# Hybrid conv and neighbourhood-attention layer on one core: weights planned one projection ahead, attention in 48 groups of four blocks

## The chip, the core and the metric

The kernel runs on one core of a Trainium2 chip. The metric is the device time of one execution in microseconds (us). TensorE is called PE here, VectorE DVE, ScalarE ACT, GpSimd POOL, and SyncE, which issues most of the transfers, SP.

## The reference, cut to what matters

One layer on 512 prompt tokens and 1024 sample tokens (d = 1024), with 16 meta tokens ahead of them. The normalised input goes through one projection into seven parts; a gated depthwise convolution of 31 taps and an attention over a neighbourhood of 8 rows by 16 columns work on these, and their gated results are projected back.

```python
u = rms_norm(h, pre_g)
z = jnp.einsum('bld,de->ble', u, w_in)
c_val, c_glu, c_gate, q, k, v, a_gate = jnp.split(z, [...])
conv_out = conv_module(c_val, c_glu, ...) * silu(c_gate)   # val*sigmoid(glu) -> 31 taps -> LayerNorm -> silu
o_meta, o_grid = neighbourhood_attention(q, k, v, ...)      # softmax over window and meta keys
att = concat(o_meta, o_grid).reshape(B, L, D_ATT) * silu(a_gate)
mixed = concat([conv_out, att], -1)
return h + rms_norm(einsum('ble,ed->bld', mixed, w_out), post_g)
```

## The kernel before, in words

All operands are fp32. Projections run in fp32r with every operand split into a high part (a cast on ACT) and a low part (a difference on POOL or DVE), so each product is three matmuls: high by high, low by high, high by low. In a fp32 matmul (transposes `tp`, weighted values `po`) the trace shows two passes for each instruction.

The stages follow each other: normalisation and transposes of the input (to about 160 us), the conv stage (160 to 692), attention (to about 1235), the handover and the output stage (to 1516).

Projection weights come in sets of 128 output columns. `load_w(ec)` (L118 to L126 and the lines it calls) loads set `ec` into `wraw` (DMA on SP, L122), ACT casts it into `whi` (L115), POOL subtracts into `wlo` (L116). Each of the three has two buffers. `proj` (L133) then does 24 matmuls for up to 512 tokens: that is called a unit here. A set serves three or four units. Sets 0 to 7 are conv values, 8 to 15 conv gates (`glu`), 16 to 23 the gates of the conv branch, 24 to 31 Q, 32 to 39 K, 40 to 47 the gates of the attention branch.

In the conv stage, channel block `c` (of 8) is filtered by DVE: 30 instructions of `scalar_tensor_tensor` (L223) on `z`, each 128 x 1536, and a first one on ACT (L221). While DVE filters block `c`, PE does filler units (`v_units`, `c_gate`, `a_gate`, about 44 us of them per chunk) and then gate and value units of block `c + 1` (`conv_proj`). A chunk ends by time, so a gate's three units may be cut over two chunks. The last block, c = 7, is filtered in two parts (`LASTP`): segment 0 alone (512 wide), then segments 1 and 2 (1024 wide). After a pass, `conv_stats` makes `zc` on DVE, `zq` on ACT and sums on POOL (for c = 7's second part on DVE). Matmuls with `ones` (L423) then sum over the partitions.

Attention goes pair by pair (8 pairs of heads): K of the pair (four units, L478 to L487 split it), then for each of three token groups Q (one unit, L514, L515) and `attention`, which for each of eight query blocks does scores `ss` on PE (L548, three matmuls of high and low parts), the softmax on DVE and ACT (L556 to L561), transposes `tp` (L564), their copy `pT` (ACT, L566) and the weighted values `po` (L571). `po` of a group is one PSUM bank of eight blocks; `mo` copies it out (L574) and L575 stores it. PSUM: three banks `mm`, two `ss`, two `tp`, one `po`. `pt` has three buffers, `pT` two.

The order on each engine is not the program's: a scheduler picks among the ready instructions, earlier ones in the program first, and fixes each engine's order when the kernel is built. So the units of a later Q or K stand between the blocks of an earlier group. At the end, `mix` loads gates and results (L645, L646), makes `mh` and `ml` (L654, L655), and the output product `py` (L682) runs on weights that `load_wo` loads and splits (L616, L626, L627).

## Time and profile before

| | us |
|---|---|
| median of three runs | 1517.15 |
| the runs | 1515.48, 1517.20, 1517.15 |
| the profiled execution | 1517.83 |
| its span, first to last instruction | 1516.1 |
| PE busy | 1460.5 (96%) |
| DVE busy | 1006.9 (66%) |
| ACT busy | 585.3 (39%) |
| POOL busy | 351.4 (23%) |

PE's share is near the whole span in every stage; the other engines wait for it most of the time. To be read from the profile are therefore PE's waits with what ended each, the stages' busy times, and the starts of PE's instructions one after the other: matmuls overlap, so the price of one is the time from its start to the start of the next, and its own length in a row is longer.

### The profile page before, as it was taken

The numbers are of one execution on the slowest core, as the hardware profiler recorded it, in microseconds if no ns is written. First come the engines' busy times: TensorE is split into PE (matmuls) and PEld (weight loads), VectorE is DVE, ScalarE is ACT, GpSimd is POOL, SyncE is SP. The second block draws the span as 40 slices with busy tenths as digits, with TensorE's granted clock in tenths as the row PEclk, the third lists the DMA queues.
The fourth block names the chain that finished last, engine by engine and source line by source line (L and its number), as shares of the span: only waits on it lengthen the run. The fifth ranks groups of instructions, "written<-read, shape, count | busy, mean of one in ns | idle before, by whom it ended". The sixth has DMA issues, their size and how long they took to land.

```text
span 1516.1 us, 24156 instructions
## 1 busy us (share of the span) xinstructions
PE 1460.5 (96%) x9506; PEld 1241.3 (82%) x9506; DVE 1006.9 (66%) x1739; ACT 585.3 (39%) x1296; POOL 351.4 (23%) x258
## 2 busy tenths in 40 slices
PE   7998999999999898969999999999999979999998
PEld 6987898989988787757888888888887867888876
DVE  7699989797959698991545545546555557553442
ACT  7312121122111121112544545545544567456652
POOL 1133232233031323562121111111210002122121
PEclk9999999999999999989999999999999999999999
DMA  8013123141122131024112222212222367454542
GB/s 274 24 49 104 46 59 112 53 137 61 48 74 90 38 103 63 29 87 122 52 56 65 63 61 82 66 44 61 86 58 81 119 189 218 131 169 131 148 137 75
DMA packets 124470, 138.91 MB, mean 92 GB/s; under 512 B 8110, under 2 KB 96430, under 8 KB 124356
## 3 DMA queue, kind: packets, MB, share of 16 engines
q1 hardware_dynamic: 124356, 137.36, 29.6%
q8 instruction: 75, 1.23, 0.3%
q14 instruction: 39, 0.32, 0.1%
HBM read 99.05 MB, written 42.71 MB: 94 GB/s over the span
## 4 chain that ended last, share of the span: by engine, by line
PE 76%; DVE 9%; DMA 6%; issue 4%; POOL 2%; ACT 2%; SPq 0%; DVEq 0%; POOLq 0%; ACTq 0%
PE mm L133 49%; PE mm L286 8%; DVE z L223 5%; PE ss L548 5%; PE po L571 5%; PE tp L564 4%; PE py L682 4%; DMA mb<-std 2%; DMA mx<-zs 2%; POOL wlo L116 1%; POOL ml L655 1%; DMA yo<-in_wo 1%; DVE mx L653 1%; DVE mx L649 1%; DVE mx L648 1%
## 5 line engine op out<-in xcount | busy, mean ns | idle before, releaser
L133 PE MATMUL mm<-uw,whi 128*128 128x512 f32 (+2 forms) x2688 | 757.2, 364 | 3.2 <-ACT whi L115 3.2
L133 PEld LDWEIGHTS mm<-uw,whi 128*128 128x128 f32 x2688 | 485.1, 190 | 83.7 <-ACT whi L115 4.9
L223 DVE SCALAR_TENSOR_TENSOR z<-ub,cw_sb,z 128x1536 f32<-128x1536 f32 (+2 forms) x300 | 507.7, 1710 | 23.4 <-ACT z L221 15.2
L133 PE MATMUL mm<-uw,wlo 128*128 128x512 f32 (+2 forms) x1344 | 488.4, 364 | 18.1 <-POOL wlo L116 18.1
L133 PEld LDWEIGHTS mm<-uw,wlo 128*128 128x128 f32 x1344 | 255.6, 190 | 56.8 <-POOL wlo L116 19.1
L116 POOL TENSOR_TENSOR wlo<-wraw,whi 128x1024 fp32r<-128x1024 f32 x48 | 150.0, 3126 | 437.9 <-ACT whi L115 433.0
L682 PE MATMUL py<-uw,mh 128*128 128x512 f32 x576 | 180.0, 394 | 6.8 <-ACT mh L654 6.2
L286 PE MATMUL mm<-vh,uw 128*128 128x256 f32 x768 | 141.9, 284 | 1.1 <-ACT uw L158 0.6
L566 ACT COPY pT<-tp 108x256 f32<-108x256 f32 (+4 forms) x192 | 76.1, 425 | 153.4 <-PE tp L564 146.9
L682 PEld LDWEIGHTS py<-uw,mh 128*128 128x128 f32 x576 | 108.8, 189 | 31.1 <-ACT mh L654 6.4
L286 PEld LDWEIGHTS mm<-vh,uw 128*128 128x128 f32 x768 | 119.4, 190 | 3.3 <-ACT uw L158 1.0
L559 ACT ACTIVATE pt<-pt,sm 128x216 f32<-128x216 f32 (+4 forms) x192 | 96.9, 505 | 46.3 <-DVE sm L558 44.6
L682 PE MATMUL py<-uw,ml 128*128 128x512 f32 x288 | 113.2, 394 | 0.8 <-POOL ml L655 0.8
L556 DVE CUSTOM_DVE_ANT_0 pt<-ss,ei 128x216 f32<-128x216 f32 (+2 forms) x144 | 60.8, 439 | 77.7 <-PE ss L548 73.7
L655 POOL TENSOR_TENSOR ml<-mx,mh 128x1024 fp32r<-128x1024 f32 x22 | 54.4, 2490 | 245.5 <-ACT mh L654 245.5
L286 PE MATMUL mm<-vl,uw 128*128 128x256 f32 x384 | 108.1, 282 | 0.0
L561 DVE TENSOR_SCALAR pt<-pt,sm 128x216 f32<-128x216 f32 (+4 forms) x192 | 76.2, 397 | 5.5
L564 PE MATMUL tp<-ident,pt 128*96 128x128 f32 (+2 forms) x480 | 78.8, 282 | 0.0
L286 PEld LDWEIGHTS mm<-vl,uw 128*128 128x128 f32 x384 | 72.7, 189 | 0.8 <-issue 0.5
L115 ACT CAST whi<-wraw 128x1024 fp32r<-128x1024 f32 x48 | 50.3, 1048 | 48.9 <-PE mm L133 32.8
L571 PEld LDWEIGHTS po<-pT,vt 96*64 96x64 f32 (+1 forms) x1408 | 47.8, 137 | 23.5 <-issue 13.4
L682 PEld LDWEIGHTS py<-uw,ml 128*128 128x128 f32 x288 | 54.4, 189 | 13.6 <-POOL ml L655 1.3
(147 smaller groups left out, 1630.7 us busy)
## 6 DMA issues: line engine op xcount, KB each, us to landing
wraw<-in_w_main SPq DMA_DIRECT2D x48, 512.0 KB
xt<-in_xn SPq DMA_DIRECT2D x12, 512.0 KB
vd<-vs SPq DMA_DIRECT2D x96, 64.0 KB
zs<-zc SPq DMA_DIRECT2D x24, 256.0 KB
cgd<-ag SPq DMA_DIRECT2D x24, 256.0 KB
agd<-ag SPq DMA_DIRECT2D x24, 256.0 KB
mad<-mo SPq DMA_DIRECT2D x24, 256.0 KB
mx<-zs SPq DMA_DIRECT2D x12, 512.0 KB
```

Of the source, the lines that this page charges most:

```text
L116: eng.tensor_tensor(out=lo, in0=raw, in1=hi.bitcast(F32), op=ALU.subtract)
L133: nc.tensor.matmul(ps[:, :n], lhsT=w[:, dc, :], rhs=u[dc // 4][:, dc % 4, :], start=(dc == 0 and i == 0), stop=(dc == DC - 1 and i == 2))
L223: nc.vector.scalar_tensor_tensor(out=zv, in0=ub[:, a:b, k:k + 512], scalar=cw_sb[:, c, k:k + 1], in1=zv, op0=ALU.mult, op1=ALU.add)
L286: nc.tensor.matmul(ps[:, :256], lhsT=u[dc // 4][:, dc % 4, :], rhs=w[dc // 4][:, dc % 4, :], start=(dc == 0 and i == 0), stop=(dc == DC - ...
L548: nc.tensor.matmul(ss[:, :nk * w], lhsT=q[:, jj].rearrange("p h x -> p (h x)"), rhs=k[:, b0:b0 + nk, ra:ra + rn, :].rearrange("p b r c -> ...
L559: last[0] = nc.scalar.activation(out=pv, in_=pv, func=AF.Exp, bias=sm[:, 1:2], scale=1.0, accum_out=sm[:, 2:3])
L561: nc.vector.tensor_scalar(out=pv, in0=pv, scalar1=sm[:, 3:4], scalar2=None, op0=ALU.mult)
L564: nc.tensor.transpose(out=tp[:kt, k * 128:k * 128 + 128], in_=pv[:, k * kt:k * kt + kt], identity=ident)
L566: nc.scalar.copy(out=pT[:kt, :nt * 128], in_=tp[:kt, :nt * 128])
L571: nc.tensor.matmul(po[hs, j, :], lhsT=v, rhs=pT[:kt, k * 128 + h * 64:k * 128 + h * 64 + 64], start=(k == 0), stop=(k == nt - 1))
L655: (nc.vector if t < MLT else nc.gpsimd).tensor_tensor(out=ml, in0=mx, in1=mh.bitcast(F32), op=ALU.subtract)
L682: nc.tensor.matmul(pss[hf], lhsT=m[e // 8][:, e % 8], rhs=w[e][:, hf * 512:hf * 512 + 512], start=(e == 0 and i == 0), stop=(e == 15 and i ...
```

## The change

1. `_plan()` writes down the order of all units and from it `wseq`, the order of the weight sets. `use_w(ec)` gives set `ec` and at once calls `load_w` for the set that follows it in `wseq`, so that load, cast and split of a set stand one projection ahead in the program. All of `conv_proj`, `c_gate`, `a_gate`, `pair_proj`, `pair_q` use it. The number of buffers is as before.
2. `LASTP` is gone: c = 7 is filtered like the other blocks, one pass of 1536, and its sums are on POOL.
3. Attention is written as 48 groups (pair, token group, half) of four blocks: in step n the scores and softmax of group n, the weighted values of group n − 2 (held with `issue_after` behind the last score matmul written so far), the transposes of group n − 1, and `between`, one unit of Q, of the next pair's K, or of the last gates. `pt` has 6 buffers, `pT` 4, `sm` 8 (4 before), `raw` 2 (3 before), `mo` 1 (2 before). `msq` moved to another pool.

```diff
+def _plan():
...
+        if c < 7:
+            units += [(k, c + 1, i, 24 * (MGROUPS[i][1] - MGROUPS[i][0]) * 0.00045) for k in "gx" for i in range(4)]
+        chunks.append(units)
+    base = {"g": 8, "x": 0, "cg": 16, "ag": 40}
+    seq = [8, 0]
+    for units in chunks:
+        for kind, x, _, _ in units:
+            if kind != "v" and seq[-1] != base[kind] + x:
+                seq.append(base[kind] + x)
+    seq += [32, 24]
+    for p in range(1, NPAIR):
+        seq += [32 + p, 24 + p]
+    seq += [40 + p for p in range(NAG1, NPAIR)]
+    return first, chunks, seq + list(range(16 + NCG1, 24))
...
+    def use_w(ec):
+
+        w = ahead.pop(ec) if ec in ahead else load_w(ec)
+        i = wseq.index(ec) + 1
+        if i < len(wseq) and wseq[i] not in ahead:
+            ahead[wseq[i]] = load_w(wseq[i])
+        return w
...
-            for a, b in ((0, 3),) if c < 7 else LASTP:
-                for _ in conv_taps(c, z, a, b):
-                    yield TAP_US * (b - a) / 3
-                if c == 7:
-                    for i in range(a, b):
-                        conv_stats(c, z, i, nc.vector if b == 3 else nc.gpsimd)
+            for _ in conv_taps(c, z, 0, 3):
+                yield TAP_US
...
+    def between(p, i):
+
+        if i in (0, 2):
+            pair_q(p, i // 2 + 1)
+        elif p == NPAIR - 1:
+            next(rest, None)
+        elif i == 5:
+            pair_q(p + 1, 0)
+        else:
+            if i == 1:
+                knext[0] = pair_proj(p + 1)
+                next(knext[0])
+            next(knext[0])
...
+    groups = [(p, g, hf) for p in range(NPAIR) for g in range(3) for hf in range(2)]
+    for n in range(len(groups) + 2):
+        if n < len(groups):
+            p, g, hf = groups[n]
+            if (g, hf) == (0, 0) and p > 0:
+                e_build(p)
+            scores(p, g, hf)
+        else:
+            next(rest, None)
+        if n >= 2:
+            with tc.issue_after(last_qk[0].ins):
+                weighted(*groups[n - 2])
+        if 0 <= n - 1 < len(groups):
+            transposes(*groups[n - 1])
+        if n < len(groups):
+            between(p, g * 2 + hf)
+    for _ in rest:
+        pass
```

`scores`, `transposes` and `weighted` hold the lines of the old `attention` unchanged, each as a loop over four blocks.

What this does to the order on the engines, at three places. A row is a line, an operation, its tiles and shape; the numbers in names tell tiles apart. Lines of the kernel after are its own: its cast is L148, `proj` L177, `sg` L235, `ag` of the attention gate L359, `z` L265, `zq` L289, `ss` L598, `tp` L620, `po` L636.

First place: ACT near the end of pass c = 5, where the gate units of block 6 give way to its value units. In the kernel before, `whi_4439` is the cast of the value weights, `whi_4586` that of the next attention gate:

```order
L191 ACTIVATE sg0_4323<-mm_4298 128x272 [waits PE_49]
L191 ACTIVATE sg1_4352<-mm_4327 128x256 [waits PE_49]
L191 ACTIVATE sg2_4380<-mm_4355 128x512 [waits PE_49]
L191 ACTIVATE sg3_4410<-mm_4385 128x512 [waits PE_49]
L115 CAST whi_4439<-wraw_4437 128x1024 [waits DMAHW1_49,Pool_49]
L245 ACTIVATE zq_4415<-zc_4412 128x512 [waits DVE_49]
L245 ACTIVATE zq_4422<-zc_4419 128x512 [waits DVE_49,Pool_49]
L245 ACTIVATE zq_4429<-zc_4426 128x512 [waits DVE_49,Pool_49]
L115 CAST whi_4586<-wraw_4584 128x1024 [waits DMAHW5_49,PE_49]
L221 ACTIVATE z_4551<-ub0_129,cb_sb_96,cw_sb_95 128x1536 [waits DVE_49,Pool_49]
L315 COPY ag_4577<-mm_4552 128x512 [waits DMAHW6_49,PE_49]
```

In the kernel after, the value weights are `whi_4299`; `whi_4444` is the second copy of set 40, `whi_4591` is set 41:

```order
L235 ACTIVATE sg1_4357<-mm_4332 128x256 [waits PE_49]
L235 ACTIVATE sg2_4385<-mm_4360 128x512 [waits PE_49]
L148 CAST whi_4299<-wraw_4297 128x1024 [waits DMAHW5_49,PE_49,Pool_49]
L235 ACTIVATE sg3_4415<-mm_4390 128x512
L289 ACTIVATE zq_4420<-zc_4417 128x512 [waits DVE_49]
L289 ACTIVATE zq_4427<-zc_4424 128x512 [waits DVE_49,Pool_49]
L289 ACTIVATE zq_4434<-zc_4431 128x512 [waits DVE_49,Pool_49]
L148 CAST whi_4444<-wraw_4442 128x1024 [waits DMAHW5_49,PE_49]
L265 ACTIVATE z_4556<-ub0_128,cb_sb_95,cw_sb_94 128x1536 [waits DVE_49,Pool_49]
L148 CAST whi_4591<-wraw_4589 128x1024 [waits DMAHW1_49,Pool_49]
L359 COPY ag_4582<-mm_4557 128x512 [waits DMAHW6_49,PE_49]
L148 CAST whi_4597<-wraw_4595 128x1024 [waits DMAHW4_49]
```

The cast of the value weights moved ahead of `sg3`; it waits for PE, and `sg3` behind it waits for nothing more. The cast of the second copy of set 40 is new, and that of set 41 stands behind it and behind a POOL operation.

Second place: PE in attention, end of one pair and start of the next. Before:

```order
L571 MATMUL po<-pT,vt 64x64 x6
L564 MATMUL tp<-ident,pt 104x128 x3
L548 MATMUL ss<-kl,qh_5542 128x256
L548 MATMUL ss<-kh,ql_5543 128x256
L133 MATMUL mm<-uw,whi 128x272
L133 MATMUL mm<-uw,wlo 128x272
L133 MATMUL mm<-uw,whi 128x272
L571 MATMUL po<-pT,vt 64x64 x6
L564 MATMUL tp<-ident,pt 104x128 x3
L548 MATMUL ss<-kh,qh_5530 128x264
L548 MATMUL ss<-kl,qh_5530 128x264
L548 MATMUL ss<-kh,ql_5531 128x264
```

After:

```order
L598 MATMUL ss<-kh,qh_5522 128x312
L598 MATMUL ss<-kl,qh_5522 128x312
L598 MATMUL ss<-kh,ql_5523 128x312
L636 MATMUL po<-pT,vt 64x64 x22
L598 MATMUL ss<-kh,qh_5528 128x312
L598 MATMUL ss<-kl,qh_5528 128x312
L598 MATMUL ss<-kh,ql_5529 128x312
L598 MATMUL ss<-kh,qh_5528 128x312
L598 MATMUL ss<-kl,qh_5528 128x312
L598 MATMUL ss<-kh,ql_5529 128x312
L620 MATMUL tp<-ident,pt 96x128 x5
L177 MATMUL mm<-uw,whi 128x256
```

Six matmuls of one block, or ten to twelve of two, stood in a row of weighted values before; now the 22 of four blocks stand in one, between scores, and the transposes stand apart.

Third place: SP at the handover, the stores of the last weighted values (`mad2`) and the first loads of output weights (`in_wo`) and of operands of `mix`. Before:

```order
L616 DMA xr_12150<-in_wo 128x1024 [waits DMAHW1_49,PE_49]
L616 DMA yo_12155<-in_wo 128x1024 [waits DMAHW2_49]
L667 DMA pgb_12232<-in_postg 128x1024 [waits DMAHW3_49]
L645 DMA mx_12073<-zs0_57 128x8x128 [waits DMAHW4_49,DVE_49]
L645 DMA mx2_12080<-mad0_63 128x8x128 [waits DMAHW5_49,DVE_49]
L616 DMA xr_12170<-in_wo 128x1024 [waits DMAHW6_49,DMAHW1_49,DVE_49]
L616 DMA yo_12175<-in_wo 128x1024 [waits DMAHW7_49,DMAHW2_49,DVE_49]
L616 DMA wraw_12180<-in_wo 128x1024 [waits DMAHW0_49,DVE_49]
L616 DMA wraw_12186<-in_wo 128x1024 [waits DVE_49]
```

After:

```order
L744 DMA mx2_12061<-mad0_63 128x8x128 [waits DMAHW7_49,DMAHW2_49,DMAHW0_49]
L745 DMA gt2_12062<-agd0_66 128x8x128 [waits DMAHW1_49]
L715 DMA xr_12131<-in_wo 128x1024 [waits PE_49]
L715 DMA yo_12136<-in_wo 128x1024 [waits DMAHW3_49]
L744 DMA mx_12053<-zs0_57 128x8x128 [waits DMAHW4_49,DVE_49]
L766 DMA pgb_12213<-in_postg 128x1024 [waits DMAHW5_49]
L745 DMA gt2_12062<-agd0_66 128x8x128 [waits DMAHW6_49,DVE_49]
L715 DMA xr_12151<-in_wo 128x1024 [waits DMAHW2_49,DVE_49]
L744 DMA mx2_12061<-mad0_63 128x8x128 [waits DMAHW0_49,DVE_49]
L715 DMA yo_12156<-in_wo 128x1024 [waits DMAHW3_49,DMAHW1_49,DVE_49]
```

Behind the last `mad2` store the loads `mx2` and `gt2` now stand ahead of `xr` and `yo`; they stood elsewhere before, `mx2` behind them.

## Rows read from the trace of the kernel before

**Rows 1.** conv stage and attention: us, then each engine's busy time and count
```profile
160.00:692.00 532.00, 510.70 (x2899) 446.97 (x2899) 453.59 (x286) 97.23 (x158) 175.73 (x95) 0.97 0.23 73
...
724.00:1235.00 511.00, 508.70 (x4401) 428.65 (x4399) 276.50 (x1130) 261.54 (x754) 70.71 (x79) 1.00 0.24 72
```

**Rows 2.** waits of PE, longest sums first: us in total, times, longest us
```profile
PE mm L133 <- POOL wlo L116: 18.1, 3, 13.0
...
PE mm L133 <- ACT whi L115: 3.2, 2, 1.6
```

**Rows 3.** PE's timeline at 591 us: start, length, operation, count, [idle before <-releaser]
```profile
591.43 0.39 PE L133 MATMUL mm<-uw,whi 128*128 128x512 f32 x1
...
596.77 0.60 PE L133 MATMUL mm<-uw,wlo 128*128 128x272 f32 x1 [2.59 <-POOL wlo L116]
```

**Rows 4.** ACT's timeline, the cast at 592 us
```profile
592.35 1.04 ACT L115 CAST whi<-wraw 128x1024 fp32r<-128x1024 f32 x1
```

**Rows 5.** PE's timeline at 643 to 657 us
```profile
656.60 0.80 PE L133 MATMUL mm<-uw,wlo 128*128 128x512 f32 x1 [13.03 <-POOL wlo L116]
657.19 1.06 PE L133 MATMUL mm<-uw,whi 128*128 128x512 f32 x2
```

**Rows 6.** the page, granted clock of TensorE in 40 slices, in tenths
```profile
PEclk9999999999999999989999999999999999999999
```

**Rows 7.** POOL's timeline, splits of weights in the conv stage
```profile
554.70 2.75 POOL L116 TENSOR_TENSOR wlo<-wraw,whi 128x1024 fp32r<-128x1024 f32 x1 [14.10 <-ACT whi L115]
571.17 3.19 POOL L116 TENSOR_TENSOR wlo<-wraw,whi 128x1024 fp32r<-128x1024 f32 x1 [13.72 <-ACT whi L115]
...
628.51 28.03 POOL L116 TENSOR_TENSOR wlo<-wraw,whi 128x1024 fp32r<-128x1024 f32 x1 [8.29 <-ACT whi L115]
```

**Rows 8.** DVE's timeline, taps of c = 6 and c = 7
```profile
533.81 64.52 DVE L223 SCALAR_TENSOR_TENSOR z<-ub,cw_sb,z 128x1536 f32<-128x1536 f32 x30 [1.91 <-ACT z L221]
...
617.24 36.50 DVE L223 SCALAR_TENSOR_TENSOR z<-ub,cw_sb,z 128x512 f32<-128x512 f32 x37
...
654.25 21.73 DVE L223 SCALAR_TENSOR_TENSOR z<-ub,cw_sb,z 128x1024 f32<-128x1024 f32 x12
```

**Rows 9.** PE's timeline, first matmul of the statistics
```profile
691.39 1.02 PE L423 MATMUL ss<-acc,ones 128*1 128x512 f32 x2
```

**Rows 10.** PE's timeline in attention, pair p = 3
```profile
927.93 0.69 PE L571 MATMUL po<-pT,vp 108*64 108x64 f32 x16
...
949.53 0.62 PE L133 MATMUL mm<-uw,whi 128*128 128x512 f32 x2
...
950.21 0.39 PE L133 MATMUL mm<-uw,whi 128*128 128x512 f32 x1
950.53 0.92 PE L571 MATMUL po<-pT,vt 96*64 96x64 f32 x24
951.38 0.86 PE L564 MATMUL tp<-ident,pt 128*96 128x128 f32 x6
...
967.49 0.41 PE L548 MATMUL ss<-kh,qh 128*128 128x312 f32 x1
...
969.84 0.29 PE L133 MATMUL mm<-uw,whi 128*128 128x272 f32 x1
969.96 0.49 PE L564 MATMUL tp<-ident,pt 128*104 128x128 f32 x3
970.21 0.37 PE L133 MATMUL mm<-uw,whi 128*128 128x272 f32 x1
```

**Rows 11.** the page, groups: operation xcount | busy, mean ns | idle before
```profile
L566 ACT COPY pT<-tp 108x256 f32<-108x256 f32 (+4 forms) x192 | 76.1, 425 | 153.4 <-PE tp L564 146.9
```

**Rows 12.** PE's timeline at the handover to the output stage
```profile
1223.61 0.28 PE L548 MATMUL ss<-kh,ql 128*128 128x256 f32 x1
...
1234.21 0.80 PE L571 MATMUL po<-pT,vt 104*64 104x64 f32 x20 [1.70 <-ACT pT L566]
1241.26 2.08 PE L682 MATMUL py<-uw,mh 128*128 128x512 f32 x4 [6.25 <-ACT mh L654]
```

More of the change, by code (lines that the diff above doesn't have):

```diff
@@ L47 @@
 NXT = 4
-LASTP = ((0, 1), (1, 3))
 LAG = 1
@@ L51 @@
 TAP_US = 1.85
+def _plan():
+    fill = []
+    for qv in range(4):
+        fill += [("v", qv, t, 2.8) for t in range(12)]
+        fill += [("cg", qv, g, 5.5) for g in range(3)]
+    fill += [("cg", c, g, 5.5) for c in range(4, NCG1) for g in range(3)]
+    fill += [("ag", p, g, 5.5) for p in range(NAG1) for g in range(3)]
+    first, fill = fill[:NVS], fill[NVS:]
+    chunks = []
+    for c in range(8):
+        t, units = 0.0, []
+        while fill and t < FILL[c]:
+            units.append(fill.pop(0))
+            t += units[-1][3]
+        if c < 7:
+            units += [(k, c + 1, i, 24 * (MGROUPS[i][1] - MGROUPS[i][0]) * 0.00045) for k in "gx" for i in range(4)]
+        chunks.append(units)
+    assert not fill
+    base = {"g": 8, "x": 0, "cg": 16, "ag": 40}
[9 more added lines that the diff above has]
+    return first, chunks, seq + list(range(16 + NCG1, 24))
 CONV_ORDER = tuple((k, i) for k in "gv" for i in range(4))
@@ L295, in c_gate @@
     def c_gate(cs):
-        ws = [load_w(16 + c) for c in cs]
+        ws = [use_w(16 + c) for c in cs]
         if cs[0] < 3:
@@ L373, in stream @@
     def stream(c):
[L375 to L380 removed]
+        conv = conv_proj(c + 1, CONV_ORDER) if c < 7 else None
+        for kind, _, _, dt in chunk_units[c]:
+            next(conv if kind in "gx" else fill)
             yield dt
[L382 to L383 removed]
     def convolve(c, z):
         if c > 0:
[L388 to L393 removed]
+            for _ in conv_taps(c, z, 0, 3):
+                yield TAP_US
         else:
             conv_mean(z)
[L396 to L399 removed]
+        for i in range(3):
+            conv_stats(c, z, i, nc.gpsimd)
+            yield TAP_US / 3
         if 1 <= c <= 6:
@@ L561, in attention, with transposes @@
             nc.vector.tensor_scalar(out=pv, in0=pv, scalar1=sm[:, 3:4], scalar2=None, op0=ALU.mult)
+            pts[p, g, j] = pv
+    def transposes(p, g, hf):
+        for j in range(hf * 4, hf * 4 + 4):
+            _, _, _, nt, kt, _ = block(g, j)
+            pv = pts.pop((p, g, j))
             tp = ps_t.tile([128, 512], F32, name="tp")
@@ L575, in attention @@
-        nc.sync.dma_start(mad[g][p], mo)
-    for p in range(NPAIR):
-        e_build(p)
-        kh, kl = pair_proj(p)
-        wqh, wql = load_w(24 + p)
-        for g in range(3):
-            qs = pair_q(p, wqh, wql, g)
-            attention(p, g, kh, kl, qs)
-        if p >= NAG1:
-            for _ in a_gate(p):
-                pass
-    for cs in [(c,) for c in range(NCG1, 6)] + [(6, 7)]:
-        for _ in c_gate(cs):
-            pass
+        if hf == 1:
+            mo = apool.tile([128, 512], F32, name="mo", bufs=1)
+            nc.vector.tensor_copy(out=mo, in_=pos.pop((p, g)).rearrange("p j x -> p (j x)"))
+            nc.sync.dma_start(mad[g][p], mo)
@@ new lines, in last_gates @@
+    def last_gates():
+        for p in range(NAG1, NPAIR):
+            yield from a_gate(p)
+        for cs in [(c,) for c in range(NCG1, 6)] + [(6, 7)]:
+            yield from c_gate(cs)
+    rest = last_gates()
+    def between(p, i):
[10 more added lines that the diff above has]
+            next(knext[0])
@@ L590, in tile_encoder @@
+    for _ in rest:
+        pass
     es2.close()
```

122 lines of the change are left out of this document (66 added, 56 removed).

## The prediction

> **What bounds the kernel now.** I read the stages first. TensorE (PE) works 510.70 of the 532 us of the conv stage and 508.70 of the 511 us of attention [rows 1]. So PE is the bound, and a change can pay in two ways only: PE waits less, or PE's own work gets shorter. Attention has no waits to give (2.3 us idle in 511), the conv stage has 21.
>
> The waits of PE say where these are: 18.1 us in three waits for POOL's `wlo`, 3.2 us in two for ACT's `whi` [rows 2]; the handover to the output stage is taken up in part D. In order of time:
> - Near 509 and near 595, one pattern. PE starts a unit's last matmul at 591.43, waits for the cast, does three short matmuls, waits for the split (2.59 us) and goes on at 596.77 [rows 3]: 5.34 us, less the 0.6 that these four matmuls need, some 4.8 us lost; near 509 it is 4.7. The cast starts at 592.35 [rows 4], when the gate unit before has ended: the weights of value, conv gate and an attention gate that is cut over the chunk's end are three sets, and there are two buffers.
> - At 643: 13.03 us of idleness for `wlo` [rows 5], and behind it PE's clock is at the lower of its two levels for a moment: two matmuls of 512 take 1.06 us instead of 0.62, and the granted clock of that slice of the page is the one below 0.9 [rows 5, 6]. Some ten matmuls at 0.43 instead of 0.23 from start to start add 2.2 us: 15.2 in all. The POOL operation took 28.03 us, where its kind took 2.75 and 3.19 in earlier passes [rows 7]. What differs is VectorE (DVE): for c = 7 it runs two interleaved chains of taps, 37 without a gap from 617.24 [rows 8], while pass c = 6 is one chain (30 taps in 64.52 us), and there POOL gets in between two taps.
>
> **Part A, conv stage.** (1) `LASTP` goes, c = 7 becomes one pass like c = 6. The wait at 643 then goes: −15.2 (cover: splits of 2.8 to 3.2 us, each cast a unit ahead of use, as the one at 571.17 [rows 7], behind which PE had no wait; a unit of 24 matmuls is 24 × 0.227 = 5.4 us). (2) "One projection ahead" doesn't reach the waits at 509 and 595. ACT's order in the changed kernel still has the value weights `whi_4299` and `whi_4832` waiting for PE, and the `sg3` behind them has no wait of its own: the PE event awaited is the end of the gate unit, as before. They only come ahead of `sg3` (0.5 us): −1.0 for both. (3) The plan names codes 40 and 43 a second time, since an attention gate is cut over the chunk's end; `use_w` so loads and splits two sets that no matmul reads (512 KB, a cast of 1.04, a split of some 2.75 us each), and codes 41 and 44 are loaded at their own use. For 41, the chain cast, split, cast, split is 2 × (1.04 + 2.75) = 7.6 us against one unit of 5.4: +2.2. For 44 two units cover it: 0. (4) c = 7's pass starts when its last segment is there, at 617.3, and ACT has made the first `z` (1.9 us of waiting for that in pass c = 6): about 619. At c = 6's length, 64.5 us, it ends near 684 instead of 676.0 (654.25 + 21.73 [rows 8]); `zc` and POOL's sums follow, to some 690. PE does the statistics' matmuls at 691.4 now [rows 9]; in its new order they stand some 10 us of projection matmuls later, and A's other terms bring it there 14 earlier: 687.5. So what is late next is DVE's last pass: +2.5, between 0 and 8. Sum of A: −15.2 − 1.0 + 2.2 + 2.5 = **−11.5**, from −15 to −4.
>
> On (1) a rule of the Trainium skill speaks against the change (page "SBUF — State Buffer", section "SBUF: two separate sides"): a DVE instruction with two SBUF inputs takes the port pair that it shares with GpSimd for its whole length, and the loser blocks fully. The taps are such instructions; where they follow each other without a gap, POOL would get nothing until the pass ends. The row of 28.03 us agrees with that; the rows of 2.75 and 3.19, inside a running pass, show POOL let in after one tap. The result by that rule is rival 4.
>
> **Part B, PE's work in attention.** The same matmuls are issued, but the weighted values (`po`) of four blocks stand together: in PE's order there are 120 runs of `po` before and 50 after, 70 fewer. What a run costs besides its matmuls: three projection matmuls start within 950.21 − 949.53 = 0.68, so 0.227 each; from the last to the run's start it is 0.32: +0.09. The run itself: 0.69 for 16 and 0.92 for 24, so 0.0288 each; from its start to the transposes 951.38 − 950.53 = 0.85 are 24 × 0.0288 and 0.16 more [rows 10]. Behind it, a transpose run brings nothing more that it would not cost elsewhere, a score matmul some 0.1 (at 967.49, 312 wide, 0.41; at 1223.61, 256 wide, 0.28, of which the width is some 0.03). So 0.25 for a run left to transposes and 0.35 for one left to scores. 70 × 0.25 = 17.5; of the runs left to scores there are 10 before and 16 after, 6 × 0.1 = 0.6 back: **−17**. Transposes now stand in more runs (some 205 instead of 132); a run of three inside matmuls takes 970.21 − 969.96 = 0.25 and the matmul behind it 0.37 instead of 0.29, some 0.11 per transpose, and four behind a `po` run are no cheaper: 0. Bounds: 70 × 0.16 = 11 if the entry is paid anyway, 70 × 0.30 = 21.
>
> **Part C, waits in the new order.** PE runs in order: where a `po`, `tp` or `ss` waits, the projection matmuls behind it wait too. Between a score and its transposes PE has at least 4.8 us of other work in the new order (3.3 before), between scores that share a bank 1.15 (1.2), between transposes and the `po` that reads them 0.9 (1.4), between transposes that share a bank 0.6 to 0.9 in eight places (1.07). These are sums of slots, against a `pT` copy of 0.43 us [rows 11]. `issue_after` holds a `po` run behind the scores of the group two further on; its `pT` are long there. I take +1.5 (48 groups, a few tenths in some), from 0 to +6. A gain is excluded but for what A and B count: only 2.3 us are idle.
>
> **Part D, handover.** PE's last score is at 1223.61; behind it stand 9.5 us of work, a wait of 1.70 for `pT` and one of 6.25 for `mh` [rows 12]. In the new order there are some 14.7 us behind the last score, since the last gates stay back as filler: 5 of those 8 us are filled. But on the DMA queue (SP) two loads of output weights (`xr`, `yo`) now stand behind the loads `mx2` and `gt2`, the first of which waits for three DMA counts; about 2 us given back: **−3**, from −6 to +3.
>
> Sum, on the profiled execution's 1517.83 (0.7 over the median of 1517.15): −11.5 − 17 + 1.5 − 3 = −30, so **1488**.
>
> **The rivals.**
> 1. The plan does what its words say, and all three weight waits go: −15.2 − 4.8 − 4.7 + 2.5 = −22.2 in A, −40.7 in all: 1477. For it: the weights are asked for earlier in the program. Against: ACT's order, which has the value cast wait for PE, and two buffers for three sets. 0.12.
> 2. The conv gain is given back at its end. If the single pass meets more POOL work than c = 6 did (the statistics too are POOL's now), or K's evacuation, which stands behind `zc` on DVE, holds PE's banks, the wait of (4) becomes 10 to 12: 1496. For it: PE and DVE end this stage within 3 us of each other by the sum. 0.15.
> 3. The new order waits in attention: a quarter of a microsecond at each of 48 groups' short places (transposes on the same bank, `pT` to `po`) takes 12 of the 17 us: 1499. Against: half a microsecond of slack at the shortest place. 0.13.
> 4. Slower: POOL is shut out of c = 7's pass. It starts at 619 and, if no POOL work gets in, ends some 56 us later (64.5 less about 2 for each of the four splits in pass c = 6). The split that is needed near 628.5 then comes at about 678: a wait of 49 us, with 2 us of low clock behind it, in place of 15.2, and none at the statistics. A would be +37, the sum +18: 1536. It decides from a wait of some 32 us, since the other terms bring 17. For it: the 28.03 us. Against: all single-chain passes let POOL in. 0.04.
>
> **How the numbers follow.** The forecast, 1488, has 0.56; its own range is 1478 to 1497 by the bounds of A to D. The range of 8 in 10 takes rivals 1 to 3 in almost whole: 1475 to 1503. This measurement can tell about 0.2% (3 us) from no change. Faster by more than that: all but rival 4 and mishaps of two kinds together, 0.93; within it 0.03; slower 0.04.
>
> **What would show it.** (1) right: no POOL split over 4 us between 620 and 685, no PE wait for `wlo` near 643. (2) right: PE's waits for cast and split near 509 and 595 of 4 us still there, and a new one of one to three for `wlo` near 540, at the first unit of code 41. (4): a PE wait of up to 8 us at the statistics, with the last tap near 684. B: attention from first score to last `po` shorter by 15 to 18, with `po` runs of 32 and 44 passes. C: PE waits for `pT` or `tp` in the waits' view under 2 us in sum. D: `mh` wait near 3. The forecast fails if POOL's splits in c = 7 are long, if attention shows waits per group, or if a `po` run's price lies in its matmuls and not in its ends.

## The result and the profile after

The changed kernel takes 1495.34 us (median of four runs, 1493.83 to 1495.75), the kernel before 1517.02 beside it: a ratio of 0.9857, 95% interval 0.984 to 0.9875. The forecast was 1488, with a range of 1475 to 1503. So the direction and the range hold, and of the 30 us that were forecast some 22 came.

The page of the kernel after, its span and its first part (busy time of each engine, share of the span, instructions):

```profile
span 1493.8 us, 24010 instructions
...
PE 1449.1 (97%) x9506; PEld 1240.1 (83%) x9506; DVE 1005.6 (67%) x1705; ACT 599.3 (40%) x1301; POOL 338.6 (23%) x264
```

The stages, as in [rows 1] (length, busy time and count of PE, PEld, DVE, ACT, POOL, then PEclk, DMA share, GB/s); attention now ends near 1209:

```profile
160.00:692.00 532.00, 520.38 (x2960) 454.38 (x2959) 451.12 (x257) 100.09 (x161) 159.22 (x99) 0.99 0.24 77
...
724.00:1210.00 486.00, 482.77 (x4320) 417.45 (x4319) 279.48 (x1100) 264.12 (x737) 70.23 (x78) 1.00 0.25 75
1210.00:1240.00 30.00, 21.60 (x74) 14.95 (x73) 19.99 (x16) 18.26 (x23) 5.78 (x2) 0.84 0.93 287
```

PE's idle time in the conv stage is 11.6 us instead of 21.3. In the 30 us of the handover, a stretch that the prediction priced with a gain, it is busy for 21.6 only, at a granted clock of 0.84 on the mean, part of it at the lower of its two levels (1.2 and 2.4 GHz), behind the waits shown below. The waits of PE (us in total, times, longest), of which [rows 2] has the first two of before:

```profile
PE mm L177 <- POOL wlo L149: 6.5, 3, 3.0
PE py L781 <- DVE uw L726: 5.0, 3, 3.8
PE py L781 <- ACT uw L725: 3.4, 2, 2.6
...
PE mm L177 <- ACT whi L148: 2.4, 2, 1.2
...
PE ss L457 <- POOL acc L290: 1.5, 1, 1.5
PE tp L620 <- ACT pT L622: 1.2, 1, 1.2
```

The wait of 13.0 for `wlo` is gone, the pairs near 509 and 595 are still there, and at the output products there are 8.4 us of waits for casts and splits of output weights (`uw`), where the kernel before had 1.6.

Where the 22 us come from is read best from the starts of the same PE instructions in both traces. PE does the same units in the same order in the conv stage, so each stretch can be compared; in attention only the ends can.

| stretch (PE, from start to start) | before | after | difference | forecast |
|---|---|---|---|---|
| up to the unit before the wait at 509 | 496.4 | 496.6 | +0.2 | 0 |
| four units with the wait at 509 | 23.7 | 24.2 | +0.4 | −0.5 |
| four units with set 41 | 21.8 | 23.4 | +1.6 | +2.2 |
| twelve units with the wait at 595 | 63.1 | 62.7 | −0.4 | −0.5 |
| eight units with the wait at 643 | 58.9 | 43.7 | −15.2 | −15.2 |
| from there to the first score | 62.2 | 64.0 | +1.8 | +2.5 |
| first score to first output product | 515.1 | 494.8 | −20.4 | −20.5 |
| first to 97th output product | 25.8 | 36.9 | **+11.1** | **+2** |
| the rest | 242.1 | 240.9 | −1.1 | 0 |

The forecast of the third line from the end is B (−17), C (+1.5) and the 5 us of D that were to fill idle time. Every line but one is within 1.1 us of its step. What is missing was given back in one place, behind the first output product.

### The profile page after: what moved, and what is told of

Same layout as the page of the kernel before. It is cut to its first block, busy times and chain, and to the rows that moved or that the text cites. A ratio compares the mean times of both kernels' runs of the same rounds, so it can differ in the third digit from the quotient of the medians.

```text
span 1493.8 us, 24010 instructions
## 1 busy us (share of the span) xinstructions
PE 1449.1 (97%) x9506; PEld 1240.1 (83%) x9506; DVE 1005.6 (67%) x1705; ACT 599.3 (40%) x1301; POOL 338.6 (23%) x264
## 4 chain that ended last, share of the span: by engine, by line
PE 74%; DVE 19%; ACT 2%; DMA 2%; POOL 1%; issue 1%; SPq 0%; DVEq 0%; ACTq 0%; POOLq 0%
PE mm L177 39%; DVE z L267 17%; PE py L781 17%; PE ss L598 5%; PE mm L330 5%; PE po L636 4%; PE tp L620 3%; POOL wlo L149 1%; DMA mb<-std 1%; DMA wraw<-in_w_main 1%; DMA xr<-in_wo 0%; ACT whi L148 0%; DVE uw L726 0%; DVE zc L284 0%; PE ss L457 0%
## 5 line engine op out<-in xcount | busy, mean ns | idle before, releaser
L177 PE MATMUL mm<-uw,whi 128*128 128x512 f32 (+2 forms) x2688 | 759.8, 365 | 3.3 <-ACT whi L148 2.4
L177 PEld LDWEIGHTS mm<-uw,whi 128*128 128x128 f32 x2688 | 481.4, 190 | 82.3 <-issue 3.7
L177 PE MATMUL mm<-uw,wlo 128*128 128x512 f32 (+2 forms) x1344 | 490.0, 365 | 6.5 <-POOL wlo L149 6.5
L177 PEld LDWEIGHTS mm<-uw,wlo 128*128 128x128 f32 x1344 | 255.0, 190 | 46.2 <-POOL wlo L149 7.5
L149 POOL TENSOR_TENSOR wlo<-wraw,whi 128x1024 fp32r<-128x1024 f32 x50 | 135.6, 2713 | 380.9 <-ACT whi L148 379.0
L781 PE MATMUL py<-uw,mh 128*128 128x512 f32 x576 | 183.2, 399 | 8.4 <-DVE uw L726 5.0
L622 ACT COPY pT<-tp 108x256 f32<-108x256 f32 (+4 forms) x192 | 79.4, 424 | 63.4 <-PE tp L620 51.3
L620 PE MATMUL tp<-ident,pt 128*96 128x128 f32 (+2 forms) x480 | 87.7, 275 | 1.5 <-ACT pT L622 1.2
L148 ACT CAST whi<-wraw 128x1024 fp32r<-128x1024 f32 x50 | 52.5, 1049 | 69.8 <-PE mm L177 64.5
L610 DVE RECIPROCAL sm<-sm 128x1 f32<-128x1 f32 x192 | 31.3, 163 | 71.1 <-ACT pt L609 68.4
L556 DVE SCALAR_TENSOR_TENSOR ql<-mm,qh 64x256 fp32r<-64x256 f32 x96 | 40.3, 420 | 47.5 <-ACT qh L555 46.0
```

The source lines that it names most:

```text
L149: eng.tensor_tensor(out=lo, in0=raw, in1=hi.bitcast(F32), op=ALU.subtract)
L177: nc.tensor.matmul(ps[:, :n], lhsT=w[:, dc, :], rhs=u[dc // 4][:, dc % 4, :], start=(dc == 0 and i == 0), stop=(dc == DC - 1 and i == 2))
L620: nc.tensor.transpose(out=tp[:kt, k * 128:k * 128 + 128], in_=pv[:, k * kt:k * kt + kt], identity=ident)
L622: nc.scalar.copy(out=pT[:kt, :nt * 128], in_=tp[:kt, :nt * 128])
L781: nc.tensor.matmul(pss[hf], lhsT=m[e // 8][:, e % 8], rhs=w[e][:, hf * 512:hf * 512 + 512], start=(e == 0 and i == 0), stop=(e == 15 and i ...
```

## The experiments

Each kernel was run beside the kernel before on the same chip. Ratios are to that, with their 95% interval.

| kernel | us | ratio |
|---|---|---|
| the change | 1495.34 | 0.9857 [0.984, 0.9875] |
| one_chain | 1503.78 | 0.9917 [0.99, 0.9933] |
| attn_only | 1507.93 | 0.9939 [0.9924, 0.9955] |
| at_use | 1492.62 | 0.9838 [0.9823, 0.9853] |
| whole_gates | 1485.79 | 0.9788 [0.9771, 0.9804] |
| two_runs | 1502.85 | 0.9905 [0.989, 0.992] |
| msq_ones | 1496.34 | 0.9863 [0.9849, 0.9878] |
| both | 1490.42 | 0.9819 [0.9804, 0.9834] |
| msq_held | 1495.73 | 0.9859 [0.9842, 0.9877] |
| both_held | 1486.82 | 0.9811 [0.9782, 0.984] |
| half_bytes | 1496.10 | 0.9862 [0.9847, 0.9877] |
| tail_wg | 1482.25 | 0.9774 [0.9758, 0.9791] |
| tail_held | 1482.06 | 0.9769 [0.9754, 0.9783] |

Whole times are the medians. Stretches are from the profiled executions, which for whole_gates and both_held lie 3.6 and 7.9 us above the median, for both_held nearly all of it ahead of the conv stage's second half; so no whole is taken from them.

### The taps of c = 7 in one chain (one_chain)

The kernel before, with one line and the engine of the sums changed:

```diff
-LASTP = ((0, 1), (1, 3))
+LASTP = ((0, 3),)
```

> The kernel before with one line edited: the taps of c = 7 in one pass of three segments, its sums on POOL. Theory (two interleaved chains shut POOL out for 28 us, one chain lets it in): the wait of 13.0 at 643 and the slow matmuls behind it go, 15.2 us; PE waits some 2 us at the statistics; together 12 to 14 us less than before, 1503 to 1505 us; no split over 4 us. Rival (POOL is shut out by any back-to-back taps with two SBUF inputs): the split takes 28 us or more, 1517 us or more.

1503.78 us, 12.6 less than the kernel before beside it. POOL's timeline in that pass:

```profile
644.68 2.74 POOL L116 TENSOR_TENSOR wlo<-wraw,whi 128x1024 fp32r<-128x1024 f32 x1 [14.12 <-ACT whi L115]
661.15 3.19 POOL L116 TENSOR_TENSOR wlo<-wraw,whi 128x1024 fp32r<-128x1024 f32 x1 [13.73 <-ACT whi L115]
677.63 3.57 POOL L116 TENSOR_TENSOR wlo<-wraw,whi 128x1024 fp32r<-128x1024 f32 x1 [13.29 <-ACT whi L115]
```

These splits answer to the one of 28.03 us of [rows 7]: they took 2.74 to 3.57 us with the taps running on one side of them and on the other. PE's waits for `wlo` fell from 18.1 us to these:

```profile
PE mm L133 <- POOL wlo L116: 5.1, 2, 2.6
```

So step (1) of part A is shown alone: the stall was made by two interleaved chains. The rival that POOL is shut out of any pass of back-to-back taps falls. The edit also makes the taps wider (1536 instead of 512 and 1024), but that isn't the reason: in the kernel before, the split of 28.03 us ends at 656.54, 2.3 us behind the point from which only the chain of 1024 is left (654.25 in [rows 8]), and the next split, inside that single chain, is short:

```profile
663.21 3.27 POOL L116 TENSOR_TENSOR wlo<-wraw,whi 128x1024 fp32r<-128x1024 f32 x1 [6.66 <-ACT whi L115]
```

In the records a tap of a single chain starts some 0.04 us behind the end of the one before it; a tap of the two interleaved chains starts 0.09 us ahead of that end.

### Attention's order alone (attn_only)

The changed kernel with two chains again, and with `use_w` loading ahead only for Q and K:

```diff
-            for _ in conv_taps(c, z, 0, 3):
-                yield TAP_US
+            for a, b in ((0, 3),) if c < 7 else ((0, 1), (1, 3)):
...
-        if i < len(wseq) and wseq[i] not in ahead:
+        if i < len(wseq) and wseq[i] not in ahead and ec >= 24 and ec < 40:
```

> The changed kernel with its conv stage put back: two chains for c = 7, and in the conv stage each weight set loaded at its first use; the 48 groups and the order of attention stay. Theory (the parts add): the conv stage is as before with its waits of 4.7, 4.8 and 15.2; from the first score to the first output product 20 us less than before, of which 11 are given back in the first 96 output products: 8 to 11 us less than before, 1506 to 1509 us. Rival (attention gains by weights that are planned ahead across stages, or the give-back belongs to the conv gain): the whole 20 remain, 1497 to 1499 us, or nothing does.

1507.93 us, 8.5 less than before. The conv stage is that of the kernel before (first score at 726.16 in both); from the first score to the first product it is 494.6 us (515.1 before), from there to the 97th 38.9 (25.8 before). PE's waits show both ends:

```profile
PE mm L177 <- POOL wlo L149: 18.1, 3, 13.0
...
PE py L786 <- DVE uw L731: 7.4, 4, 6.1
...
PE py L786 <- ACT uw L730: 3.2, 2, 2.4
```

The 13.0 is back, and the waits for `uw` are there without the conv gain. The parts add: 12.6 and 8.5 make 21.1, and the whole change brought 21.7. The give-back of 11 to 13 us belongs to attention's part, not to the conv gain.

### No projection ahead (at_use)

```diff
-        if i < len(wseq) and wseq[i] not in ahead:
+        if False:
```

> The changed kernel with each weight set loaded at its first use, not one projection ahead. Theory (the loads of the kernel before were early enough, and the waits left are those of two buffers): the waits near 509 and 595 stay, the one of 1.65 at set 41 goes, no new ones come; 0 to 3 us less than the changed kernel, 1492 to 1496 us. Rival (loading ahead carries a part of the gain): 1500 us or more, with waits of PE for cast or split in attention.

1492.62 us: 2.7 less than the change, in the direction and size of step (3), though the two intervals overlap. Loading a projection ahead, which the change is named for, carries none of the gain; with it go the second copies of sets 40 and 43 and the wait at set 41. PE's waits for weights are then those of before at 509 and 595 and no others:

```profile
PE mm L177 <- POOL wlo L149: 5.0, 2, 2.6
...
PE mm L177 <- ACT whi L148: 3.2, 2, 1.6
```

### Gates not cut over a chunk's end (whole_gates)

```diff
-FILL = (0, 44, 44, 44, 44, 44, 44, 999)
+FILL = (0, 44, 44, 44, 44, 32, 32, 999)
```

> The changed kernel with one line edited: the fifth and the sixth chunk take six filler units instead of eight, so no attention gate is cut over a chunk's end, no weight set stands twice in the plan, and at the turn from gate to value units three sets no longer share two buffers. Theory (the waits near 509 and 595 are those of a cut gate): both waits of 4.7 and 4.8 us go, the new one of 1.65 at set 41 goes, and the wait of some 2 us at the statistics too, since the last pass of taps starts earlier: 11 to 13 us less than the changed kernel, 1482 to 1485 us. Rival (these waits are the price of any split beside DVE's taps at the turn to a new block, cut gate or not): they stay, 0 to 2 us less, 1493 to 1495 us.

1485.79 us: 9.6 less than the change. PE at the turn to value units in the change, near 509, 540 and 595 (start, length, operation, count, idle before and what ended it):

```profile
508.84 1.00 PE L177 MATMUL mm<-uw,whi 128*128 128x272 f32 x3 [1.18 <-ACT whi L148]
512.47 0.59 PE L177 MATMUL mm<-uw,wlo 128*128 128x272 f32 x1 [2.63 <-POOL wlo L149]
```

```profile
539.22 0.51 PE L177 MATMUL mm<-uw,wlo 128*128 128x512 f32 x1 [0.91 <-POOL wlo L149]
```

```profile
595.25 1.00 PE L177 MATMUL mm<-uw,whi 128*128 128x272 f32 x3 [1.18 <-ACT whi L148]
599.22 0.59 PE L177 MATMUL mm<-uw,wlo 128*128 128x272 f32 x1 [2.98 <-POOL wlo L149]
```

The pairs at 508.84 and 595.25 are the pattern of [rows 3], 539.22 is the new wait of step (3). With whole gates the same turn reads (the second row holds the last matmul of the gates and the first of the values):

```profile
495.08 0.39 PE L177 MATMUL mm<-uw,wlo 128*128 128x512 f32 x1
495.31 0.51 PE L177 MATMUL mm<-uw,whi 128*128 128x512 f32 x2
495.65 0.30 PE L177 MATMUL mm<-uw,wlo 128*128 128x272 f32 x1
```

There is no wait in it, and no line of PE's waits names `wlo` or `whi` any more. The first score comes 10.1 us earlier than in the change (9.1, when the 0.9 are left out by which this execution was ahead at unit 36). The cut gate is shown as the cause, and the rival (any split beside the taps) falls. That two buffers for three sets are how it acts follows from the order on ACT; a third buffer was not tried. The gain is less than the 11 to 13 us that were expected: PE now waits 3.0 us for `ub`, the gated values, instead of 0.7, and 3.2 at the statistics instead of 1.5. At the handover some of it went again: the first 96 products took 40.6 us in the profiled execution.

### Weighted values in two runs (two_runs)

```diff
             with tc.issue_after(last_qk[0].ins):
-                weighted(*groups[n - 2])
+                weighted(*groups[n - 2], 0)
...
+        if n >= 2:
+            with tc.issue_after(last_mm[0].ins):
+                weighted(*groups[n - 2], 1)
```

> The changed kernel with the weighted values of a group issued in two parts, two blocks before the transposes and the projection unit and two behind them; PE's order then has 109 runs of them instead of 50, with the same matmuls. Theory (a run costs 0.25 us besides its matmuls: 0.09 at its start, 0.16 at its end): 59 x 0.25 = 15 us more, about 1510 us, without new waits of PE. Rival (the price lies in the matmuls, and attention got shorter by something else, waits or transposes): 0 to 3 us more, 1495 to 1498 us.

From the first score to the first output product it is 509.29 us instead of 494.75: 14.5 us for 59 runs more, 0.246 each, the price of part B (0.29 by PE's busy time, since PE's idle time in that stretch is 2.4 us less). But the whole is 7.5 us longer, not 15, since the first 96 products then take 30.6 us instead of 36.9: some 7 us of the last gates' matmuls now stand behind the last weighted values, and what that is worth is shown below (tail_held). A run of the changed kernel and two of this one:

```profile
1180.83 1.50 PE L636 MATMUL po<-pT,vt 96*64 96x64 f32 x44
1182.26 0.41 PE L598 MATMUL ss<-kh,qh 128*128 128x312 f32 x1
```

```profile
950.23 0.80 PE L638 MATMUL po<-pT,vt 104*64 104x64 f32 x20
950.97 0.54 PE L622 MATMUL tp<-ident,pt 128*104 128x128 f32 x3
951.43 0.92 PE L638 MATMUL po<-pT,vt 104*64 104x64 f32 x24
```

From 1180.83 to 1182.26 it is 1.43 us for 44: 44 × 0.0288 + 0.16, as in [rows 10]. Behind the run the first score is 0.41 long, as at 967.49 before. So B's price is shown: it lies at the ends of a run, not in its matmuls.

### The order on SP at the handover (msq_ones, both)

The change moved `msq` (512 bytes) from one pool to another, and with it `mx2`, `gt2` and the rest of that pool 512 bytes down. In the built program `mx2` then lies at 207328 to 211424 (bytes of a partition) and `mo`, the tile of the weighted values on their way out, at 205600 to 207648: 320 bytes are shared. Before, `mx2` lay over a tile of Q and none of `mo`. So the load of `mx2` (L744) now waits until the last store of `mo` has landed. SP's waits at the handover name it (us in total, times, longest):

```profile
SPq L744 <- DMA mad<-mo: 1.7, 1, 1.7
```

SP goes through its queue in order:

```profile
1210.18 0.33 SPq L641 DMA_DIRECT2D mad<-mo  x1
1212.26 0.37 SPq L744 DMA_DIRECT2D mx<-mad  x1
1212.68 0.57 SPq L745 DMA_DIRECT2D gt<-agd  x1
1213.31 1.27 SPq L715 DMA_DIRECT2D xr<-in_wo  x1
```

The store is issued at 1210.18, `mx2` 2 us later, and the first of the output weights (`xr`) at 1213.31. The edit, in msq_ones alone and in both together with whole gates:

```diff
-    msq = mp1.tile([128, 128], F32, name="msq")
+    msq = ones
```

> The changed kernel with the 512-byte buffer msq left out (its values go into the constant ones, which nothing reads any more by then). In the changed kernel msq moves mx2 down so that it overlaps mo by 320 bytes; mx2's load then waits for the last store of mo to land, and the loads of the output weights stand behind it on SP. Without the overlap the order on SP is that of the kernel before again. Theory (the 11 us given back after the first output product come from that order): from the first to the 97th output product 31 to 33 us instead of 36.9, the whole 4 to 8 us less, about 1489 us. Rival (the DMA engines are full there, so an order among the loads changes nothing): 0 to 2 us less, 1493 to 1495 us.

> Both edits of the two runs beside this one together. Theory: they lie in different stages and add, 15 to 20 us less than the changed kernel, 1475 to 1480 us, less than either alone. Rival (what the conv stage gains is waited for again in attention or at the handover): 1483 us or more.

SP's order is then as before, `xr` right behind the store:

```profile
1216.45 0.33 SPq L641 DMA_DIRECT2D mad<-mo  x1
1216.87 0.38 SPq L715 DMA_DIRECT2D xr<-in_wo  x1
```

And the first 96 products take 30.9 us instead of 36.9, as expected. Yet the whole is 1496.34, no less than the change, and both together are 1490.42, where the rival had put it and more than whole_gates alone. The 6 us came back ahead of the first product: from the first score to it, it is 503.2 us instead of 494.8.

```profile
1213.11 0.67 PE L620 MATMUL tp<-ident,pt 128*104 128x128 f32 x2 [5.63 <-ACT pT L622]
...
1215.61 2.08 PE L781 MATMUL py<-uw,mh 128*128 128x512 f32 x4
```

```profile
1207.19 1.28 ACT L738 ACT_TABLE_LOAD   x1 [0.80 <-DMA mb<-std]
...
1212.57 0.86 ACT L622 COPY pT<-tp 104x384 f32<-104x384 f32 x2
```

PE's transposes wait 5.63 us for a `pT`, and on ACT the copies `pT` at 1212.57 stand behind work of the second mix that had waited for its load (`mb`) and ran from 1207.19 on. That makes up 4.6 us of the 8.4 (from the last score to the last weighted values it is 22.4 instead of 17.8); the other 3.7 are told in the next section. My expectation took the stretch alone and was right on it; on the whole it failed.

### That mix held behind the last copy (msq_held, both_held)

```diff
         if e == EM1:
-            mix(1)
+            with tc.issue_after(last_pt[0].ins):
+                mix(1)
```

> The changed kernel with msq left out and the second mix held behind the last copy pT, the conv stage as in the changed kernel. Theory of two orders: 1489 to 1492 us, 4 to 6 us less than the changed kernel. Rival (DMA engines full): 1494 to 1497 us, no change against the changed kernel.

> The run of both edits with a third: the second mix of the output stage is held behind the last copy pT. In the run of both edits the saved 6 us behind the first output product came back ahead of it: on ACT the last copies pT stood behind an activation of that mix that waits for a transfer, and PE waited 6.0 us for them. Theory (two orders share one loss: SP's order behind the products, ACT's ahead of them): PE's wait for pT falls under 2 us, the time from last weighted values to the 97th product stays at 31 to 33 us, and the sum is 4 to 6 us less than both edits, 1484 to 1487 us. Rival (the DMA engines are what is full at the handover, and whatever comes ready earlier waits for them): from last weighted values to the 97th product it grows to 36 us or more, 1488 to 1491 us.

1495.73 and 1486.82 us. In the first, where the rival had put it, nothing is won against the change; the second is 3.6 less than both by the medians, but by the ratios only 1.2, within the intervals; so a gain of the hold isn't shown. PE still waits for a `pT`, 3.45 us instead of 5.63:

```profile
1210.15 0.67 PE L621 MATMUL tp<-ident,pt 128*104 128x128 f32 x2 [3.45 <-ACT pT L623]
```

In msq_ones, both, msq_held and both_held the stretch from the 481st score matmul to the last is 3.7 us longer too (84.9 instead of 81.2), with a wait of 2 us of a score for DVE in it. That doesn't hold for every kernel without `msq`: it is 83.8 in half_bytes and 81.6 in tail_held. The order of the last pair's work on ACT and DVE differs there from the change's; which row costs what was not taken apart.

### What sets the pace behind the last weighted values (half_bytes)

| kernel | last score to last `po` | `po` to first product | first to 97th | last `po` to 97th | ninth load behind the first product |
|---|---|---|---|---|---|
| before | 11.2 | 6.5 | 25.8 | 32.3 | −0.1 |
| one_chain | 11.2 | 6.2 | 26.3 | 32.5 | −0.1 |
| the change | 17.8 | 0.2 | 36.9 | 37.1 | 4.0 |
| attn_only | 17.6 | 0.2 | 38.9 | 39.1 | 4.0 |
| at_use | 17.5 | 0.2 | 37.2 | 37.4 | 4.0 |
| whole_gates | 17.8 | 0.2 | 40.6 | 40.8 | 4.7 |
| two_runs | 25.5 | 7.3 | 30.6 | 37.9 | −1.8 |
| msq_ones | 22.4 | 0.2 | 30.9 | 31.1 | 1.3 |
| both | 22.8 | 0.2 | 32.2 | 32.5 | 1.3 |
| msq_held | 20.3 | 0.2 | 30.6 | 30.9 | 2.3 |
| both_held | 20.0 | 0.2 | 32.3 | 32.5 | 2.3 |
| half_bytes | 20.4 | 0.2 | 31.8 | 32.0 | 2.3 |
| tail_held | 15.8 | 12.8 | 22.1 | 34.9 | −10.3 |
| tail_wg | 15.4 | 15.8 | 22.1 | 37.9 | −11.6 |

The last column is the time at which SP gives out the ninth of the 16 loads of output weights, the first `xr`, counted from the first product; the first eight are given out at least 8 us ahead of that product.

From the last weighted values to the 97th product it is 31 to 32.5 us wherever SP's order is that of before and no gates stand behind the last weighted values, whether PE is idle for 6 us ahead of the first product or not at all. PE's work in it is 22.1. So something other than PE sets that stretch. That the sums agree doesn't show one cause, though: before, the ninth load is given out 6.4 us behind the last `po`, and the 97th product starts 25.9 us after it; in msq_ones these are 1.5 and 29.6. What the rows do show is how the first 96 products go with this load: they take 22.1 us where it goes 10 us or more ahead of the first product, 26 to 32 where it goes between 2 us ahead and 2 us behind, and 37 to 41 where it goes 4 to 5 us behind. The transfers were the first suspect:

```diff
-        nc.sync.dma_start(raw, wo[e])
+        half = e >= 6
+        nc.sync.dma_start(raw[:, :D // 2] if half else raw, wo[e][:, :D // 2] if half else wo[e])
...
+            twice = raw[:, :D // 2].unsqueeze(1).broadcast_to([128, 2, D // 2])
```

> The changed kernel with msq left out and the second mix held, in which the output weights 6 to 15 are loaded by half (256 KB instead of 512 KB each); cast and split work on the half twice, so ACT, DVE and PE do as much as before, on other numbers. Some 2 MB less stand behind the last weighted values. Theory (from the last weighted values to the 97th product the transfers set the pace, 31 us): 24 to 27 us, and the whole 4 to 7 us less than the same kernel with whole loads (1495.7), 1489 to 1492 us. Rival (the orders of ACT and DVE set the pace): 30 us or more, 1494 us or more.

32.0 us, and 1496.10 for the whole. The theory fails: 2.5 MB less (ten loads of 256 KB instead of 512) move nothing. The windows of msq_held and half_bytes (columns as above; the DMA share is the last but one):

```profile
1225.00:1230.00 5.00, 5.00 (x24) 3.97 (x22) 3.66 (x4) 0.69 (x1) 0.00 (x0) 1.00 0.97 324
1230.00:1235.00 5.00, 2.71 (x10) 1.34 (x8) 4.82 (x3) 5.00 (x11) 3.00 (x1) 1.00 0.98 307
```

```profile
1225.00:1230.00 5.00, 5.00 (x23) 4.11 (x22) 5.00 (x6) 4.31 (x5) 0.33 (x1) 1.00 0.63 187
1230.00:1235.00 5.00, 4.20 (x19) 3.12 (x19) 5.00 (x4) 5.00 (x11) 2.14 (x1) 1.00 0.70 215
```

With whole loads the DMA engines are at 0.97 and 0.98 of their time; with half of them at 0.63 and 0.70, but DVE is then busy for all of the 10 us (5.00 of 5 in both), with splits and the second mix, and ACT for 9.3. Transfers and splits may lie close together as limits; the run doesn't say what each would give alone, and what sets the pace stays open.

### Work of PE behind the last weighted values (tail_held, tail_wg)

If that stretch doesn't depend on PE, then gate units that PE does ahead of the last weighted values cost their full time, and the same units behind them cost nothing. The last two units (10.9 us) moved:

```diff
         else:
-            next(rest, None)
+            for _ in range(n - len(groups) + 1):
+                next(rest, None)
...
-    for _ in rest:
-        pass
+    with tc.issue_after(last_po[0].ins):
+        for _ in rest:
+            pass
```

> The run of three edits (whole gates, no msq, second mix held) with two of the last gate units, 10.9 us of PE, put behind the last weighted values. Theory (what PE does ahead of the last weighted values doesn't shorten the 31 us behind them, what it does behind them lies beside the transfers): from the last weighted values to the 97th product 33 to 36 us, from the last score to the last weighted values 8 to 12 us instead of 20; the sum 4 to 9 us less than the same without, 1478 to 1483 us. Rival (the gates behind the last weighted values push all transfers and casts back by as much): 1485 us or more.

> The run of whole gates alone with the same two gate units put behind the last weighted values; mx2 still overlaps mo, and SP's order is that of the changed kernel. Theory: as in the run beside it, 3 to 8 us less than whole gates alone, 1478 to 1483 us. Rival: 1485 us or more.

1482.06 and 1482.25 us, 13 less than the change and 35 less than the kernel before. Against the same kernels without this edit it is 4.8 (both_held) and 3.5 (whole_gates) by the medians, 6.4 and 2.1 by the ratios, whose intervals touch in the first case and overlap in the second. The profiled executions of whole_gates and tail_wg show where it lies: their first scores are 0.03 us apart (704.55 and 704.58), what follows the 97th product is equally long, and between the two tail_wg is 7.7 us shorter (the execution of whole_gates being 3.6 above its median). PE in tail_held, last weighted values, first product, 97th:

```profile
1195.45 1.98 PE L638 MATMUL po<-pT,vt 104*64 104x64 f32 x32
...
1209.90 0.73 PE L786 MATMUL py<-uw,mh 128*128 128x512 f32 x2 [0.89 <-ACT ag L349]
...
1232.02 0.62 PE L786 MATMUL py<-uw,mh 128*128 128x512 f32 x2
```

The two units lie between 1197.4 and 1209.0, PE waits 0.9 us behind them, and from the first product to the 97th it is 22.1 us without a wait. Without filler the last groups wait for their `pT`, 4.2 us:

```profile
PE po L638 <- ACT pT L624: 4.2, 1, 4.2
```

so not all of the 10.9 is won, and the last weighted values come 15.8 us behind the last score, not the 8 to 12 that were expected. In tail_wg, with SP's order of the change, the same 22.1 us follow: there the order on SP costs nothing, since PE has other work.

## Why the prediction was right where it was, and the step that failed

**Part A was right in sum and nearly in each step**: −11.6 against −11.5. Step (1), −15.2, came to the tenth (one_chain shows it alone). Step (2), that loading ahead doesn't reach the waits at 509 and 595, holds; the half microsecond that I gave each came at one of them only. Step (3), the second copies of sets 40 and 43, cost 1.6 (2.2 were forecast), and at_use and whole_gates, each with 48 of these loads instead of 50, are faster, at_use by less than the intervals tell apart. Step (4): the pass started at 620.5 and took 66.49 us, so it ended at 687.0, not 684 (five of its taps meet a split of weights and take 3.83 us instead of 1.82; in pass c = 6 of before it was four):

```profile
620.50 66.49 DVE L267 SCALAR_TENSOR_TENSOR z<-ub,cw_sb,z 128x1536 f32<-128x1536 f32 x30 [1.90 <-ACT z L265]
```

and PE waited 1.5 for the statistics, with 1.8 in all to the first score.

The rule of the Trainium skill that spoke against step (1) (page "SBUF — State Buffer", section "SBUF: two separate sides": the loser of the shared port pair blocks for the whole instruction) doesn't decide it. The splits inside that pass:

```profile
646.84 2.91 POOL L149 TENSOR_TENSOR wlo<-wraw,whi 128x1024 fp32r<-128x1024 f32 x1 [13.94 <-ACT whi L148]
...
679.78 3.74 POOL L149 TENSOR_TENSOR wlo<-wraw,whi 128x1024 fp32r<-128x1024 f32 x1 [13.12 <-ACT whi L148]
```

They took 2.91 to 3.74 us, against 2.36 for the shortest split of this kernel: POOL lost one tap at most, not the pass. With the 28.03 us of [rows 7] the rule agrees if POOL lost to one tap after the other; what it leaves open is who gets the pair next, and there one chain of dependent taps and two independent ones differ.

**Parts B and C were right together**: from the first score to the first product −20.4 against −20.5, the 5 us of D in both. two_runs gives B's price as 0.246 to 0.29 us a run, so 17 to 20 for 70. C's waits are 0.8 us for scores and 2.1 for `pT`, the latter at the handover.

**Part D failed, in its size and its sign**: −3 was forecast, between −6 and +3, and what came is the −5 of filled idle time and +11.1 behind it, some +6. The step that failed is "5 of those 8 us are filled". I took PE's idle time ahead of the first product for a loss that PE work could fill from in front. But the filler stands ahead of the last weighted values, so it puts these off (17.8 us behind the last score instead of 11.2), and with them the last eight loads of output weights: the ninth is given out 22.0 us behind the last score instead of 17.6, and 4.0 us behind the first product instead of beside it. The first product came earlier, its weights did not. The idle time of 6.25 us [rows 12] went from ahead of the first product to between the products. From the first product to the 97th, before and after (columns as in the windows above):

```profile
1241.26:1267.09 25.83, 24.20 (x96) 18.98 (x97) 20.65 (x19) 19.94 (x26) 5.47 (x2) 0.94 0.98 309
```

```profile
1209.34:1246.24 36.90, 28.50 (x99) 20.51 (x97) 25.29 (x22) 24.09 (x30) 5.78 (x2) 0.83 0.91 276
```

Of the 11.1 us, 6.8 are waits (8.4 instead of 1.6); 4.3 are PE's busy time, 28.50 us instead of 24.20 for the same products at a mean granted clock of 0.83 instead of 0.94. The second term of D, 2 us for SP's order, was mis-sized: 37.1 instead of 31 to 32 from the last weighted values to the 97th product, so 5 to 6 in that stretch; no run shows the whole shorter by it (msq_ones 1496.34). The row that showed it stood in the order that I quoted (`mx2` waiting for three DMA counts); I had not asked what it waits for.

**The rivals.** The first (all three waits go) is out: the pairs at 509 and 595 are in the trace. The second and third put their 8 to 11 us of give-back at the statistics and in attention; they had the size and the wrong places. That the time lies in the range owes something to luck: it had been widened for these rivals, and the shortfall came at a place that neither names. The fourth, POOL shut out, is out by the splits above.

## What to carry to other kernels

Idle time ahead of a stage that loads its own operands is best filled with work that stands behind the event which lets these loads go: filler ahead of that event put the loads off here, and two units of projection moved from ahead of it to behind it brought 3.5 to 4.8 us by the medians. Ask of a plan that promises operands one step ahead how many sets are alive at each turn, not how early they are asked for: at two turns where three sets met two buffers, waits of 4.7 us stayed whatever the loads' distance, and one line about where a chunk ends removed them. And when a buffer changes its pool, look at what its neighbours lie upon then.

## What was not expected of the hardware

A split on POOL can wait for 28.03 us while DVE runs two interleaved chains without a gap, and for one tap when it runs a single chain of the same instructions; in the single chain each split costs DVE one tap of 3.83 us instead of 1.82. And the time lost at the handover isn't in the waits alone: the first 96 products take 22.1 us in tail_held and 36.9 in the change, of which 8.4 are waits; the other 6.4 are longer work of PE, 28.5 us busy at a mean granted clock of 0.83 in the change, 22.1 at 1.00 in tail_held.
